# Gate projections: four of eight k pairs of the second column group in the 7-product form, and the pairs' weight sums ordered behind the sums read from PSUM

## The chip, the cores and the metric

The kernel runs on one core of one Trainium2 chip. The metric is the device time of one execution in microseconds (us). Engines are named as in the profile: PE is TensorE's matmul, PEld its weight load, DVE is VectorE, ACT is ScalarE, POOL is GpSimd and SP is SyncE. "L307" is line 307 of the kernel before.

## The reference

One residual block works on 256 rows of 2048 columns. What matters here is the combined input projection and its last 4096 columns, the two gates:

```python
h = rmsnorm(x, g_mix[i])
proj = h @ w_in[i]
q_sb, k_sb, v_sb, q_ca, k_ca, v_ca, gate_sb, gate_ca = jnp.split(proj, splits, axis=-1)
...
merged = (jax.nn.sigmoid(gate_sb) * (y_sb @ w_sb_out[i])
          + jax.nn.sigmoid(gate_ca) * (y_ca @ w_ca_out[i]))
x = x + merged @ w_mix_out[i]
```

Everything is float32. Attention, SwiGLU and a further projection follow and are not touched.

## The kernel before

**Products.** Each operand is split into a high part "hi" (a rounded copy) and a low part "lo" (what the rounding left). A product is three matmuls of 128x512 (hi by hi, hi by lo, lo by hi), all recorded at line 307 (`three`). ACT makes the high part with a cast (L277 for a single weight piece, L292 and L295 for the two pieces of a pair); DVE makes the low part with a subtraction. All of DVE's weight subtractions are recorded at L257 (`minus`).

**Units.** A unit is two column groups of 512 columns by 16 k tiles, that is 8 k pairs. Its order is a tuple of numbers. `i, i` means that k pair i is done as two single pieces (one for each column group, 12 matmuls each, 24 in all). `-i` means that k pair i is done for both column groups at once in the 7-product form (Strassen's and Winograd's way to multiply 2x2 blocks), which takes 21 matmuls. For that, `split_pair` makes weight sums: from two raw weight tiles DVE makes t3, the difference written back into raw, t2 and t4 (four subtractions of 128x512; t2, t3 and t4 lie in "xf"), then two low parts of 128x1024 and the low part of xf (128x1536, "T" or "room"); ACT makes two casts of 128x1024 and one of xf (128x1536, L298). Four of the seven products go to PSUM banks of their own ("su"). Behind the last pair `mid` reads them: a copy of one bank on ACT (L852) and four additions on DVE (L854). At the end of the unit `add_sums` adds the four "mm" banks (L858).

**The four units in a row.** `gate_unit` builds units that take no side tasks between their pieces. One stands alone, early (about 113 to 154 us of the trace). Four follow each other from about 252 to 423 us: A (two column groups of values, orders' entry 3), and B, C and D (the gates of column group c = 1, 2 and 3). B and C use entry 0, with pairs 2, 4 and 6 in the 7-product form; D uses entry 2, with four pairs. The early unit uses entry 1, with pairs 2, 4, 5 and 6:

```python
GATE_ORDERS = ((0, 0, 1, 1, -2, 3, 3, -4, 5, 5, -6, 7, 7), (0, 0, 1, -2, 1, -4, 3, -5, 3, -6, 7, 7),
               (0, 0, -2, 1, -4, 1, -5, 3, -6, 3, 7, 7),
               (0, 0, 1, 1, 2, 2, 3, 3, -4, 5, 5, -6, 7, 7))
```

**Buffers and order.** Raw weight tiles have five buffers and one more; SP loads them. The high and low parts have three rotating buffers each and a fourth ("hi_2459" and "lo_2460"). There is one xf. The units alternate between two sets of PSUM banks. `prefetch` splits pieces up to three ahead of the one being multiplied; `issue_after` adds an order between two instructions. A scheduler makes one fixed order for each engine from all this when the program is built, and each engine goes through its own list.

Of the kernel before, what the change touches and what calls it, by code (L numbers as in the profile page):

```python
# [12 lines left out]
ALU = mybir.AluOpType  # L13
# [6 lines left out]
D = 2048  # L20
KD = D // P
HEADS = 8
W = HEADS * P
# [8 lines left out]
NB = 512  # L32
# [20 lines left out]
def block_kernel(ctx: ExitStack, tc: tile.TileContext, x, p, w_in, w_sb_out, w_ca_out, w_mix_out,  # L53
# [18 lines left out]
    nc = tc.nc  # L72
# [101 lines left out]
    def unit(wsrc, n0s, kts, lhs, forms, ext, slots, mid, post, needs, row0=0, pairs=PAIRS, alone=None, after=None,  # L174
             order=None, seed=None):


        if alone is None:
            state["unit"] = state.get("unit", -1) + 1
        pool = state["unit"] % 2 if alone is None else alone  # L180
        g = dict(kind="unit", post=post, mid=mid, slots=slots, after=after, lhs=lhs, keep=None, forms=forms, ext=ext, pool=pool,
                 side=1 - pool, hold=alone is not None, seed=seed)
        kts = list(kts)
        if order is None:
            order = [j for i in range(len(kts) // 2) for j in ([-i] if i in pairs and i < len(kts) // 2 - 1 else [i, i])]
        taken = [-i for i in order if i < 0]
        begun = set()
        for i in order:
            own = i < 0
            i = abs(i)  # L190
            part = kts[2 * i : 2 * i + 2]
            r = (row0 + 2 * i) * P
            src = [wsrc[r : r + 2 * P, n0 : n0 + NB].rearrange("(k p) n -> p k n", p=P) for n0 in n0s]
            pc = dict(g=g, kts=part, ncol=NB, needs=[needs(kt) for kt in part])
            if own:
                pieces.append(dict(pc, src=src, pair=True, first=i == taken[0], last=i == taken[-1]))
            else:
                b = int(i in begun)
                begun.add(i)
                pieces.append(dict(pc, src=[src[b]], block=b, first=i == 0, last=2 * i + 2 == len(kts)))  # L200
# [26 lines left out]
    def load(pc):  # L227
        at = state["loaded"]
        pc["raw"] = []
        for src in pc["src"]:  # L230
            raw, dst = load_piece(src, pc["ncol"])
            pc["raw"].append(raw)
            state["raw"] += 1
            if at == 0:
                for k in range(2):
                    dma_w.dma_start(dst[:, k, :], src[:, k, :])
                continue
            if at in X_LOADS:
                with tc.issue_after(state["load"].ins):
                    load_x(X_LOADS.index(at))  # L240
            state["load"] = dma_w.dma_start(dst, src)
# [17 lines left out]
    def split(pc):  # L259
        for k in pc["needs"]:  # L260
            while k not in done:
                run_task()
        raws = pc.pop("raw")
        state["raw"] -= len(raws)
        for _ in raws:
            held.popleft()
        if pc["g"]["kind"] == "unit" and len(raws) == 2:
            return split_pair(pc, *raws)
        raw, = raws
        n = raw.shape[1]  # L270
        if pc["g"]["keep"] is None:
            hi, lo = buffers(n)
        else:
            hi, lo = (t[:, pc["kts"][0] * pc["ncol"] :][:, :n] for t in pc["g"]["keep"])
        m = n // 2 if pc is pieces[0] else n
        for c in range(0, n, m):
            state["cast"] = nc.scalar.copy(hi[:, c : c + m], raw[:, c : c + m])  # L277
            pc["split"] = minus(lo[:, c : c + m], raw[:, c : c + m], hi.bitcast(F32)[:, c : c + m])
        pc["hi"] = hi.rearrange("p (k n) -> p k n", n=pc["ncol"])
        pc["lo"] = lo.rearrange("p (k n) -> p k n", n=pc["ncol"])  # L280
# [120 lines left out]
    state = dict(loaded=0, split=0, at=0, raw=0, hl=0, ext=0, ps=ps_mm, fourth=None, ring=0, places=0, hold=False)  # L401
# [6 lines left out]
    def prefetch():  # L408
        while state["loaded"] < len(pieces) and state["raw"] + len(pieces[state["loaded"]]["src"]) <= RAW + state["places"]:
            load(pieces[state["loaded"]])  # L410
            state["loaded"] += 1
        room = 2 if state["at"] < 4 + KD // 2 else 4 if state["fourth"] is not None else 3
        while state["split"] < state["loaded"] and state["split"] <= state["at"] + 3:
            pc = pieces[state["split"]]
            if state["split"] > state["at"] and sum(map(size, pieces[state["at"] : state["split"] + 1])) > room:
                break
            behind = [started["p"]]
            if pc["g"] is pieces[4]["g"]:
                behind += started.get(pc["kts"][0] - 2, [])
            with ExitStack() as order:  # L420
                for i in behind:
                    order.enter_context(tc.issue_after(i.ins))
                split(pc)
            state["split"] += 1
# [11 lines left out]
    def flush(every=1, until=None, in_turn=False):  # L436

        n = 0
        while state["at"] < len(pieces) and (until is None or until not in done):
            pc = pieces[state["at"]]  # L440
            prefetch()
            products(pc)
            seed_next()
            state["at"] += 1
            n += 1
            if tasks and every and not state["hold"] and int(n / every) > int((n - 1) / every):
                if in_turn:
                    with tc.issue_after(state["mm"].ins):
                        run_task()
                else:  # L450
                    run_task()
# [393 lines left out]
    def gate_slots(c):  # L845
        return [gates[:, t, m, c * NB : (c + 1) * NB] for m in range(2) for t in range(NT)]

    def mid(g):

        q1, q5, q6, q7 = g["sums"]  # L850
        C = g["C"] = g["slots"]()
        nc.scalar.copy(C[0], q1)  # L852
        for i, q, j in ((2, q6, 0), (1, q7, 2), (3, q5, 1), (2, q5, 2)):
            nc.vector.tensor_tensor(C[i], q, C[j], ALU.add)  # L854

    def add_sums(g, b):
        for i in (2 * b, 2 * b + 1):
# [20 lines left out]
    def gate_unit(n0s, slots, post, order):  # L878
        pool = state["gate"] = 1 - state.get("gate", 0)
        unit(w2, n0s, range(KD), T1, lambda kt: F_gate[GATE_PAIRS.index(kt // 2)], [room[:, :3072], later_y[:, :3072]],  # L880
             slots, mid, post, hneed, alone=pool, order=GATE_ORDERS[order])
# [27 lines left out]
    gate_unit([columns(1, b) for b in range(2)], lambda: value_slots((1, 0)) + value_slots((1, 1)),  # L909
              add_values((1, 0), (1, 1)), 3)  # L910
    for c in range(1, 4):
        gate_unit([6 * W + m * D + c * NB for m in range(2)], lambda c=c: gate_slots(c), add_sums, 2 if c == 3 else 0)
    flush(None)
    state["fourth"] = None
    x_ = bp.tile([P, NT, D], F32, tag="x", name="x")
# [175 lines left out]
    for blk, nk in enumerate(FF_BLOCKS):  # L1091
        key = f"h{blk}"
        for c in range(nk // 4):
            j = k0 // 4 + c
# [127 lines left out]
```

## Time and profile before

| | |
|---|---|
| Time, median of 3 runs | 1456.28 us (1456.23 to 1456.53) |
| Profiled execution, its own time | 1455.66 us |
| Span of its trace | 1453.9 us (1.76 us lie outside the span) |
| PE busy / in the chain of work that ended last | 99% / 96% |
| DVE, PEld, ACT busy | 86%, 83%, 57% |
| Waits of PE on another engine in the whole trace | three, of 1.2, 0.4 and 0.3 us |

Matmuls are pipelined: one lasts 0.39 us in the records but the next starts 0.23 us later. DVE and ACT rows overlap in the same way by some hundredths of a microsecond, so distances here go from start to start.

### The profile page before, as it was taken

How to read it: one execution, taken by the hardware profiler on the slowest of the kernel's cores; microseconds unless marked ns; L12 is line 12 of the kernel's file. 1: busy time of each engine (PE TensorE's matmuls, PEld its weight loads, DVE VectorE, ACT ScalarE, POOL GpSimd, SP SyncE). 2: the span in 40 equal slices, each digit the busy share in tenths (PEclk: the TensorE clock that was granted, in tenths of full speed). 3: DMA queues.
4: the chain of work that ended last, by engine and by line, in shares of the span. 5: the costliest groups of instructions: out<-in, count | busy, mean ns of one | idle time of the engine just before them, and what ended most of it. 6: DMA issues, size and time to landing. Idle time of an engine off the chain costs nothing.

```text
span 1453.9 us, 18702 instructions
## 1 busy us (share of the span) xinstructions
PE 1443.5 (99%) x6837; PEld 1208.8 (83%) x6837; DVE 1249.7 (86%) x1587; ACT 829.6 (57%) x993; POOL 25.1 (2%) x44
## 2 busy tenths in 40 slices
PE   9999999999999999999999999999999999999997
PEld 7888888888888888888888888888888888888886
DVE  6979777898987767888999999999999989999785
ACT  6456555655545665555556655566655556666652
POOL 0200000000010000000000000000000000000100
PEclk9999999999999999999999999999999999999999
DMA  9866555666675655765666666666666666665871
GB/s 319 283 189 212 181 172 172 180 205 198 199 257 164 180 168 181 231 204 173 198 192 189 196 222 194 199 201 208 193 194 216 195 186 201 215 189 178 275 230 70
DMA packets 164731, 291.17 MB, mean 200 GB/s; under 512 B 9024, under 2 KB 42096, under 8 KB 164384
## 3 DMA queue, kind: packets, MB, share of 16 engines
q1 hardware_dynamic: 162528, 281.32, 62.0%
q0 software_dynamic: 2112, 8.68, 1.8%
q8 instruction: 53, 0.87, 0.2%
q14 instruction: 38, 0.31, 0.1%
HBM read 284.19 MB, written 5.77 MB: 199 GB/s over the span
## 4 chain that ended last, share of the span: by engine, by line
PE 96%; DVE 2%; DMA 1%; issue 1%; ACT 0%; DVEq 0%; SPq 0%; ACTq 0%
PE mm L307 67%; PE su L307 13%; PE mm L392 8%; PE mm L394 4%; PE tp L482 1%; DVE lo L257 1%; DMA raw<-in_w_in 1%; PE mml L307 0%; DMA raw<-in_w_ple_in 0%; PE mm L382 0%; PE xps L536 0%; DVE xf L257 0%; PE yp L709 0%; ACT hi L277 0%; PE wt L800 0%
## 5 line engine op out<-in xcount | busy, mean ns | idle before, releaser
L307 PE MATMUL mm<-hi,T 128*128 128x512 f32 x2650 | 854.6, 391 | 0.4 <-DVE v L854 0.4
L257 DVE TENSOR_TENSOR lo<-raw,hi 128x1024 fp32r<-128x1024 f32 (+1 forms) x517 | 625.1, 1221 | 121.9 <-ACT hi L277 113.0
L277 ACT CAST hi<-raw 128x1024 fp32r<-128x1024 f32 (+1 forms) x379 | 396.7, 1050 | 381.0 <-PE mm L307 257.8
L307 PEld LDWEIGHTS mm<-hi,T 128*128 128x128 f32 x2650 | 497.3, 188 | 103.0 <-issue 0.8
L307 PE MATMUL mm<-lo,T 128*128 128x512 f32 x1325 | 517.1, 391 | 0.0
L307 PEld LDWEIGHTS mm<-lo,T 128*128 128x128 f32 x1325 | 248.9, 188 | 50.7
L392 PE MATMUL mm<-T,hi 128*128 128x512 f32 x512 | 179.8, 398 | 0.0
L394 PE MATMUL mm<-T,lo 128*128 128x256 f32 x512 | 139.7, 280 | 0.0
L295 ACT CAST hi<-raw 128x1024 fp32r<-128x1024 f32 x69 | 72.7, 1053 | 76.2 <-DVE raw L257 29.5
L257 DVE TENSOR_TENSOR T<-xf,T 128x1536 fp32r<-128x1536 f32 x61 | 107.2, 1757 | 8.0 <-ACT T L298 7.2
L392 PEld LDWEIGHTS mm<-T,hi 128*128 128x128 f32 x512 | 94.6, 188 | 20.1
L257 DVE TENSOR_TENSOR xf<-raw 128x512 f32<-128x512 f32 x138 | 95.1, 689 | 13.2 <-DMA raw<-in_w_ffn_out 4.1
L394 PEld LDWEIGHTS mm<-T,lo 128*128 128x128 f32 x512 | 96.7, 189 | 2.3
L298 ACT CAST T<-xf 128x1536 fp32r<-128x1536 f32 x61 | 90.2, 1479 | 12.7 <-DVE xf L257 12.3
L292 ACT CAST hi<-raw 128x1024 fp32r<-128x1024 f32 x69 | 72.6, 1052 | 31.0 <-PE mm L307 20.5
L307 PE MATMUL mm<-T,T 128*128 128x512 f32 (+1 forms) x279 | 77.2, 371 | 0.0
L307 PE MATMUL su<-hi,T 128*128 128x512 f32 x170 | 66.1, 394 | 0.0
L307 PEld LDWEIGHTS mm<-T,T 128*128 128x128 f32 x279 | 49.3, 188 | 9.1
L854 DVE TENSOR_TENSOR C<-su,C 128x512 f32<-128x512 f32 x72 | 47.8, 686 | 0.4
L257 DVE TENSOR_TENSOR xf<-raw,xf 128x512 f32<-128x512 f32 x69 | 47.5, 689 | 0.5
L257 DVE TENSOR_TENSOR raw<-raw 128x512 f32<-128x512 f32 x69 | 47.5, 689 | 0.4
L307 PE MATMUL su<-T,FP 128*128 128x512 f32 x174 | 47.3, 389 | 0.0
(280 smaller groups left out, 1242.7 us busy)
## 6 DMA issues: line engine op xcount, KB each, us to landing
raw<-in_w_ffn_in SPq DMA_DIRECT2D x176, 512.0 KB, 4.1
raw<-in_w_in SPq DMA_DIRECT2D x160, 512.0 KB, 4.4
raw<-in_w_ffn_out SPq DMA_DIRECT2D x88, 512.0 KB, 4.4
raw<-in_w_mix_out SPq DMA_DIRECT2D x32, 512.0 KB, 4.6
raw<-in_w_ple_gate SPq DMA_DIRECT2D x32, 512.0 KB, 4.9
raw<-in_w_sb_out SPq DMA_DIRECT2D x16, 512.0 KB, 3.8
raw<-in_w_ca_out SPq DMA_DIRECT2D x16, 512.0 KB, 4.5
x<-in_x SPq DMA_DIRECT2D x4, 512.0 KB, 10.2
```

Of the source, the lines that this page charges most:

```text
L257: return nc.vector.tensor_tensor(out, a, b, ALU.subtract)
L277: state["cast"] = nc.scalar.copy(hi[:, c : c + m], raw[:, c : c + m])
L292: nc.scalar.copy(h1, raw1)
L295: nc.scalar.copy(h2, raw2)
L298: nc.scalar.copy(xh, xf)
L307: state["mm"] = nc.tensor.matmul(ps, u, v, start=first, stop=last, skip_group_check=True)
L392: nc.tensor.matmul(ps, hi[:, i, f], lhs[:, kt, :, :].rearrange("p c s -> p (c s)"), start=a, stop=False)
L394: nc.tensor.matmul(ps[:, :S], lo[:, i, f], lhs[:, kt, 0, :], start=False, stop=z)
L482: nc.tensor.transpose(ps[:, k, t * P : (t + 1) * P], src[:, t, (k0 + k) * P : (k0 + k + 1) * P], ident)
L854: nc.vector.tensor_tensor(C[i], q, C[j], ALU.add)
```

## The change

There are two edits. Line 912 gives unit B (c = 1) entry 1 of the orders in place of entry 0; C and D keep theirs. In `prefetch`, a pair of a `gate_unit` unit is issued behind `state["mid"]`, the last of `mid`'s additions that had been built by then. The order is between instructions of one engine, DVE.

```diff
@@ -417,6 +417,8 @@
             if pc["g"] is pieces[4]["g"]:
                 behind += started.get(pc["kts"][0] - 2, [])
+            if pc.get("pair") and pc["g"]["hold"] and "mid" in state:
+                behind.append(state["mid"])
             with ExitStack() as order:
@@ -851,7 +853,7 @@
         nc.scalar.copy(C[0], q1)
         for i, q, j in ((2, q6, 0), (1, q7, 2), (3, q5, 1), (2, q5, 2)):
-            nc.vector.tensor_tensor(C[i], q, C[j], ALU.add)
+            state["mid"] = nc.vector.tensor_tensor(C[i], q, C[j], ALU.add)
@@ -909,7 +911,7 @@
     for c in range(1, 4):
-        gate_unit([6 * W + m * D + c * NB for m in range(2)], lambda c=c: gate_slots(c), add_sums, 2 if c == 3 else 0)
+        gate_unit([6 * W + m * D + c * NB for m in range(2)], lambda c=c: gate_slots(c), add_sums, (0, 1, 0, 2)[c])
```

In the changed kernel L852, L854 and L858 are lines 854, 856 and 860. The lists of the engines differ from the end of A to the end of D and nowhere else. Three places follow; tile names carry buffer numbers that differ a little between the two programs.

**Place 1.** DVE at the end of unit A, before; "v" are the value tiles that A's sums go to, and the L257 rows on xf_2830, raw_2748 and raw_2746 are the weight sums of B's first pair.

```order
L257 TENSOR_TENSOR xf_2830<-raw_2748 128x512
L257 TENSOR_TENSOR lo_2779<-raw_2696,hi_2778 128x1024
L257 TENSOR_TENSOR raw_2748<-raw_2748,raw_2746 128x512
L854 TENSOR_TENSOR v_2740<-su_2645,v_2739 128x512
L257 TENSOR_TENSOR xf_2830<-raw_2748 128x512
L854 TENSOR_TENSOR v_2739<-su_2645,v_2740 128x512
L858 TENSOR_TENSOR v_2739<-mm0_2487,v_2739 128x512
L257 TENSOR_TENSOR xf_2830<-raw_2746,xf_2830 128x512
L854 TENSOR_TENSOR v_2740<-su_2644,v_2739 128x512
L854 TENSOR_TENSOR v_2740<-su_2644,v_2740 128x512
```

The same place of the changed kernel:

```order
L257 TENSOR_TENSOR lo_2779<-raw_2696,hi_2778 128x1024
L856 TENSOR_TENSOR v_2742<-su_2645,v_2741 128x512
L856 TENSOR_TENSOR v_2741<-su_2645,v_2742 128x512
L860 TENSOR_TENSOR v_2741<-mm0_2487,v_2741 128x512
L856 TENSOR_TENSOR v_2742<-su_2644,v_2741 128x512
L856 TENSOR_TENSOR v_2742<-su_2644,v_2742 128x512
L257 TENSOR_TENSOR xf_2813<-raw_2716 128x512
```

The four weight sums of B's first pair stood among the four additions and now begin behind the last of them.

**Place 2.** DVE in unit B of the changed kernel, at its second pair, k pair 4 (raw_2774, raw_2776, xf_2886); in the kernel before, unit B has its second pair later. The row lo_2944 belongs to the pair behind it, k pair 5.

```order
L257 TENSOR_TENSOR lo_2888<-raw_2774,hi_2887 128x1024
L257 TENSOR_TENSOR xf_2886<-raw_2776 128x512
L257 TENSOR_TENSOR lo_2900<-raw_2798,hi_2899 128x1024
L257 TENSOR_TENSOR raw_2776<-raw_2776,raw_2774 128x512
L257 TENSOR_TENSOR xf_2886<-raw_2776 128x512
L257 TENSOR_TENSOR lo_2944<-raw_2839,hi_2943 128x1024
L257 TENSOR_TENSOR xf_2886<-raw_2774,xf_2886 128x512
L257 TENSOR_TENSOR lo_2460<-raw_2776,hi_2459 128x1024
L257 TENSOR_TENSOR room_683<-xf_2886,room_683 128x1536
```

The low part lo_2944 of the next pair stands ahead of t4 (the last xf row) of this one.

**Place 3.** PE at the end of unit B of the changed kernel; mm_2800, mm_2826, su0_2861 and su1_2862 are B's banks and mm0_3111 is C's.

```order
L307 MATMUL su0_2861<-lo_3000,T1_71 128x512
L307 MATMUL su0_2861<-hi_2999,T1_71 128x512
L307 MATMUL mm_2800<-lo_3000,T1_71 128x512
L307 MATMUL mm_2800<-hi_2999,T1_71 128x512
L307 MATMUL mm_2826<-hi_3001,T2_72 128x512
L307 MATMUL su1_2862<-hi_3001,T2_72 128x512
L307 MATMUL mm0_3111<-hi_3065,T1_71 128x512
L307 MATMUL mm_2826<-lo_3002,T2_72 128x512
L307 MATMUL mm_2826<-hi_3001,T2_72 128x512
```

The matmul on mm0_3111, the first of unit C, stands ahead of 21 of B's; before, C's first matmul stood behind all of B's:

```order
L307 MATMUL mm_2817<-hi_2459,T1_71 128x512
L307 MATMUL mm0_3107<-hi_3061,T1_71 128x512
```

On ACT of the changed kernel, the cast that makes hi_3065 stands directly behind B's copy of su0_2861 (L854). In unit D, the four weight sums of the first pair stood among and ahead of C's additions and now begin behind the last of them; the other pairs of D follow them in the same sequence as before.

## Rows read from the trace of the kernel before

**Rows 1.** The page, parts 1 and 4: engines, and the last chain's shares.

```profile
PE 1443.5 (99%) x6837; PEld 1208.8 (83%) x6837; DVE 1249.7 (86%) x1587; ACT 829.6 (57%) x993; POOL 25.1 (2%) x44
PE 96%; DVE 2%; DMA 1%; issue 1%; ACT 0%; DVEq 0%; SPq 0%; ACTq 0%
```

**Rows 2.** The waits of PE, whole span: us, count, mean.

```profile
PE warm L580 <- POOL mhalf L108: 1.2, 1, 1.2
PE mm L307 <- DVE v L854: 0.4, 1, 0.4
PE mm L382 <- ACT hi L277: 0.3, 1, 0.3
```

**Rows 3.** Early unit, B, D: PE, PEld, DVE, ACT, POOL busy; clock, DMA share, GB/s.

```profile
108.00:153.00 45.00, 45.00 (x206) 37.41 (x205) 41.23 (x46) 23.09 (x23) 0.00 (x0) 1.00 0.71 222
298.60:340.20 41.60, 41.60 (x184) 34.45 (x185) 36.82 (x42) 23.24 (x24) 0.00 (x0) 1.00 0.64 196
381.70:422.50 40.80, 40.80 (x182) 33.79 (x181) 38.28 (x42) 21.18 (x20) 2.84 (x4) 1.00 0.67 208
```

**Rows 4.** The chain that ended last, one piece: start, length, count.

```profile
314.27 5.67 PE mm L307 x25
```

**Rows 5.** Timeline of PE, end of A and B's start: start, length, instruction.

```profile
297.79 0.39 PE L307 MATMUL mm<-hi,T 128*128 128x512 f32 x1
298.59 0.47 PE L307 MATMUL mm<-hi,T 128*128 128x512 f32 x1 [0.41 <-DVE v L854]
298.90 0.39 PE L307 MATMUL mm<-lo,T 128*128 128x512 f32 x1
...
306.63 0.62 PE L307 MATMUL mm<-hi,T 128*128 128x512 f32 x2
```

**Rows 6.** Timeline of DVE at the end of A.

```profile
294.22 0.69 DVE L257 TENSOR_TENSOR xf<-raw 128x512 f32<-128x512 f32 x1 [0.91 <-DMA raw<-in_w_in]
...
297.16 0.68 DVE L257 TENSOR_TENSOR xf<-raw 128x512 f32<-128x512 f32 x1
297.76 0.69 DVE L854 TENSOR_TENSOR v<-su,v 128x512 f32<-128x512 f32 x1
```

**Rows 7.** Timeline of ACT in B and D.

```profile
307.06 1.06 ACT L277 CAST hi<-raw 128x1024 fp32r<-128x1024 f32 x1 [1.55 <-PE mm L307]
...
322.97 1.48 ACT L298 CAST T<-xf 128x1536 fp32r<-128x1536 f32 x1 [0.57 <-DVE xf L257]
...
331.18 0.57 ACT L852 COPY gates<-su 128x512 f32<-128x512 f32 x1
331.65 1.05 ACT L277 CAST hi<-raw 128x1024 fp32r<-128x1024 f32 x1
...
392.33 1.05 ACT L277 CAST hi<-raw 128x1024 fp32r<-128x1024 f32 x1 [2.35 <-PE su L307]
393.28 1.48 ACT L298 CAST room<-xf 128x1536 fp32r<-128x1536 f32 x1
```

**Rows 8.** Timeline of DVE at the second pair of B.

```profile
321.11 1.23 DVE L257 TENSOR_TENSOR lo<-raw,hi 128x1024 fp32r<-128x1024 f32 x1 [0.16 <-ACT hi L277]
322.25 0.68 DVE L257 TENSOR_TENSOR xf<-raw,xf 128x512 f32<-128x512 f32 x1
...
324.48 1.76 DVE L257 TENSOR_TENSOR T<-xf,T 128x1536 fp32r<-128x1536 f32 x1 [0.41 <-ACT T L298]
326.16 1.22 DVE L257 TENSOR_TENSOR lo<-raw,hi 128x1024 fp32r<-128x1024 f32 x1
```

**Rows 9.** Timeline of DVE in D: first pair's first sum, C's last additions, second and fourth pair's last rows.

```profile
371.60 0.69 DVE L257 TENSOR_TENSOR xf<-raw 128x512 f32<-128x512 f32 x1 [0.31 <-DMA raw<-in_w_in]
...
381.02 1.28 DVE L854 TENSOR_TENSOR gates<-su,gates 128x512 f32<-128x512 f32 x2
...
394.79 1.76 DVE L257 TENSOR_TENSOR room<-xf,room 128x1536 fp32r<-128x1536 f32 x1 [0.15 <-ACT room L298]
...
410.64 1.75 DVE L257 TENSOR_TENSOR room<-xf,room 128x1536 fp32r<-128x1536 f32 x1
```

## Prediction

> **What bounds the kernel now.** I read the page first: PE is busy 99% of the span and holds 96% of the chain that ended last [rows 1]. The three waits of PE on another engine come to 1.9 us in all [rows 2]; so work taken from DVE or ACT gains nothing by itself, and what a change can gain is matmuls or one of these waits. One of the three lies at the edge of A and B: B's first matmul waited for an addition of A's sums [rows 2, 5]. The windows then show how thin the cover is: in B, DVE was busy 36.82 of 41.60 us, in D 38.28 of 40.80 us, and PE never waited [rows 3]. The granted clock is 1.00 throughout these windows [rows 3], the higher of its two levels, 2.4 GHz. A matmul takes 5.67 / 25 = 0.227 us from start to start [rows 4].
>
> So the question is whether the lists of DVE and ACT, in the changed order, still deliver each operand before PE comes to it. I answer it by walking the loops in the changed lists with distances from the rows.
>
> **The distances.** All are start to start or end to start.
> - From a matmul that reads a buffer last to the cast that reuses it: the third piece's last matmul began at 306.63, the cast at 307.06, so 0.43 us [rows 5, 7].
> - A cast of 128x1024 lasts 1.05 us and lets the next begin 0.95 us on (392.33 to 393.28); a copy of a bank lets the next cast begin 0.47 us on (331.18 to 331.65); the cast of xf lasts 1.48 us [rows 7].
> - On DVE a low part takes 1.14 us (321.11 to 322.25), a 128x512 row 0.60 us (297.16 to 297.76), and the low part of xf 1.68 us, with its end after 1.76 us [rows 6, 8].
> - t4's end (322.25 + 0.68 = 322.93) to xf's cast (322.97) is 0.04 us, and that cast's end (324.45) to DVE's row (324.48) is 0.03 us [rows 7, 8].
> - DVE's end to PE's start: the second addition ended at 297.76 + 0.69 = 298.45 and PE began at 298.59, so 0.14 us [rows 5, 6]. I use the same from ACT to PE, where no row stands alone.
> - A stop costs more than its length: the matmul behind the stop came 0.31 us after it (298.59 to 298.90), not 0.227, so 0.08 us on top [rows 5].
>
> **What goes away.** One more pair in the 7-product form takes 24 - 21 = 3 matmuls off, 0.68 us. The stop at the edge of A and B was 298.59 - 297.79 - 0.23 = 0.57 us, with the restart 0.65 us [rows 5]. In the changed list no weight sum stands between the first two additions any more, which brings the second one forward by at least 0.60 us (one 128x512 row), and the weight sum ahead of the first may go with it. Since 0.60 is over 0.57, I count the stop as gone: 0.68 + 0.65 = 1.33 us gained.
>
> **What DVE and ACT get.** DVE gets four rows of 128x512 and one of 128x1536, 4 x 0.60 + 1.68 = 4.08 us [rows 6, 8]; ACT gets one cast of xf, 1.48 us [rows 7]. Between nothing (hidden, as DVE was idle for 4.8 us of B's window [rows 3]) and 4.08 us, the loops decide where they show.
>
> **Four places where PE would wait.**
> 1. *B's second pair.* lo_2944 now stands ahead of t4 on DVE. Its cast needs the buffer that a single piece's last matmul frees, at T. Then cast begins at T + 0.43 and ends 1.05 later; lo 0.03 after it; t4 1.14 on, lasting 0.68; xf's cast 0.04 after, lasting 1.48; the low part of xf 0.03 after, lasting 1.76; PE 0.14 after. The sum is 6.78 us. PE has 25 matmuls queued behind T, 5.67 us. So it waits 1.11, with the restart 1.19 us.
> 2. *B's end.* C's first matmul stands ahead of 21 of B's. Its cast stands behind the copy of su0_2861, which needs the last matmul on that bank: 0.43 + 0.47 + 1.05 + 0.14 = 2.09 us. Five starts lie between, 1.13 us. The wait is 0.96, with the restart 1.04 us. Before, C's first matmul came behind all of B's, and 21 x 0.227 = 4.8 us covered the same chain.
> 3. *D's first pair.* Its first weight sum began at 371.60 and now stands behind C's last additions, which ended at about 382.2 [rows 9]: some 10 us of lead are gone. On ACT xf's cast stands behind a cast that waits for the first piece's buffer: 0.43 + 0.95 + 1.48 + 0.03 + 1.76 + 0.14 = 4.79 us against 19 matmuls, 4.31 us. The wait is 0.48, with the restart 0.56 us.
> 4. *D's third pair.* With no lead left, DVE's own work between two pairs decides: two pairs' sums (8 rows of 128x512), six low parts and two rows of 128x1536. From the second to the fourth pair of D, which is the same mix, it took 410.64 - 394.79 = 15.85 us [rows 9]; the changed list has one wait for xf's cast in it, and I take 16.0 us. PE needs 66 matmuls for this, 14.97 us. The wait is 1.03, with the restart 1.11 us.
>
> Together 1.19 + 1.04 + 0.56 + 1.11 = 3.90 us lost, 1.33 gained: 2.57 us slower. By the profiled execution that is a span of 1453.9 + 2.57 = 1456.5 us and a time of 1458.2 us; its 1455.66 lies 0.62 us under the median of the runs, and on the median it is 1456.28 + 2.57 = 1458.9 us. The bounds of this case: each loop's handovers could be off by some 0.1 to 0.2 us, which on four loops gives 1458.2 to 1460.0 us; the edge stop, if it stayed, would bring 0.65 us and lies inside.
>
> SP loads the same tiles in another order. The raw tiles of a pair are held longer when its sums begin later, so a load can come late: DVE waited 0.91 and 0.31 us for loads at B's and D's first pairs [rows 6, 9]. With those waits moved behind the additions, they should be gone; I cost them at nothing, and at most 0.91 us for a pair.
>
> The Trainium skill (Perfetto Trace Analysis, Identifying the Most-Contended Engine) says that occupancy is a fair measure for VectorE, that matmul busy time is none for TensorE, and that weight-load busy time should be taken there; by it DVE with 86% stands ahead of PEld with 83%, DVE is the engine to relieve, and the change loads it further. The trace agrees on the two shares, but not that DVE binds: PE waited for it once, 0.4 us [rows 1, 2].
>
> **The rivals.**
> - *No stop comes (the other side).* If buffers come free about 1.1 us earlier than in my loops, all four waits vanish, and 1.33 us are gained: 1455.0 us. For it: the early unit has the same order of pairs, and no wait of PE lies in it [rows 2, 3], with DVE 92% busy. Against it: there the row ahead of the second pair's t4 is a low part of that pair itself, whose cast comes earlier than the next pair's, and no such unit follows at its end. Past 0.96 us of error in loops 1 and 2, and 1.03 in 4, this decides; it also is what remains if the order edit is inert.
> - *Only B's two stops come*, since D keeps more lead than I give it: 1.19 + 1.04 - 1.33 = 0.90, 1457.2 us. For it: D's window has the highest DVE share, 94%, and PE still did not wait [rows 3].
> - *DVE binds through all of B to D*, so each microsecond that it gets shows: 4.08 - 0.68 = 3.4 us, 1459.7 us. Against it: DVE idled 4.8 us in B and 2.5 us in D [rows 3]. This is also what the skill's page cited above would lead to.
> - *Loads come late*, 0.91 us at three of the four changed pairs on top of my case [rows 6]: 1458.9 + 2.7 = 1461.6 us. Against it: DMA was busy 64 to 71% in these windows [rows 3].
>
> **How the numbers follow.** My case gets 0.60, no stop 0.18, B's stops only 0.12, DVE bound 0.07, late loads 0.03. The likeliest gives 1458.9 us, its own range 1458.2 to 1460.0. The range that takes in the other side goes from 1454.9 to 1460.2 us, since 0.18 lies at the low end and cannot be left out. A measurement of this kernel cannot tell less than about 0.2%, 2.9 us, from no change: from 1453.4 to 1459.2 us counts as the same. The most that can be gained is 1.33 us, 0.09%, so faster gets 0.01. Some 0.4 of my case lies above 1459.2 (0.24), nearly all of DVE bound (0.07) and late loads (0.03) too: slower 0.34, same 0.65.
>
> **What would show it.** In the changed trace: no wait of B's first matmul for A's additions; a wait of PE for the low part of xf (room) some 18 to 21 us into B; one for a cast on C's first matmul ahead of B's last 21; and two for room in D, 16 us apart. If DVE's t4 in B follows lo without PE waiting, loop 1 is wrong; if the first wait in D is missing, the 10 us of lead were not needed. The forecast fails if the buffers' reuse, which I read from the lists, does not bind as I walk it, or if new waits stand where I walked none.

## The result and the profile after

The changed kernel took 1458.58 us (median of 21 runs, 1457.82 to 1459.89) against 1456.18 us for the kernel before (21 runs, 1455.19 to 1457.59) on the same chip. The ratio is 1.0018, 95% interval 1.0012 to 1.0023: slower by 0.18%. The interval leaves out 1, so the change is slower, though by less than the bound of 0.2% that the prediction set for no change. Forecast were 1458.9 us, with 0.65 for the same and 0.34 for slower. The profiled execution took 1458.38 us, its span 1456.6 us.

The page of the changed kernel, parts 1 and 4; [rows 1] hold the same lines of before.

```profile
PE 1444.0 (99%) x6834; PEld 1207.6 (83%) x6834; DVE 1255.0 (86%) x1592; ACT 830.4 (57%) x994; POOL 24.8 (2%) x44
PE 97%; DVE 1%; ACT 1%; DMA 1%; issue 0%; SPq 0%; DVEq 0%; ACTq 0%
```

The waits of PE in the changed kernel, whole span; they answer to [rows 2].

```profile
PE su L307 <- DVE room L257: 1.4, 3, 0.8
PE warm L582 <- POOL mhalf L108: 1.2, 1, 1.2
PE mm L307 <- ACT hi L277: 0.7, 1, 0.7
PE mm L382 <- DVE pT L568: 0.4, 1, 0.4
PE mm L307 <- DVE lo L257: 0.3, 1, 0.3
```

The shares say little: none moved by more than a point. The waits say more. The one on A's additions is gone, and five new ones are there: three on "room" (the low part of xf), one on a cast and one on a low part. The waits at L580/L582 and L382 lie in the first ten microseconds and differ a little in every execution.

Busy times by stretch in the changed kernel, B, C and D, with the columns of [rows 3], which hold the windows of B and D before.

```profile
298.20:340.20 42.00, 40.70 (x177) 32.76 (x176) 39.17 (x43) 24.92 (x25) 0.00 (x0) 1.00 0.58 188
340.20:382.00 41.80, 41.80 (x186) 34.60 (x186) 38.40 (x44) 20.64 (x19) 0.00 (x0) 1.00 0.66 207
382.00:425.50 43.50, 42.37 (x186) 34.41 (x185) 41.82 (x46) 23.41 (x22) 2.85 (x4) 1.00 0.67 218
```

PE's busy time fell below the window's length in B and in D; DVE's rose from 36.82 of 41.60 to 39.17 of 42.00 us in B. The granted clock stayed at 1.00.

The timeline of PE in the changed kernel, the rows at its stops, with the row ahead of each where it stands alone; [rows 5] hold the stop of before.

```profile
316.08 0.39 PE L307 MATMUL su<-hi,T 128*128 128x512 f32 x1
316.75 0.50 PE L307 MATMUL mm<-lo,FP 128*128 128x512 f32 x1 [0.29 <-DVE lo L257]
317.09 0.39 PE L307 MATMUL mm<-hi,FP 128*128 128x512 f32 x1
...
318.25 0.39 PE L307 MATMUL mm<-room,T 128*128 128x512 f32 x1
318.93 0.96 PE L307 MATMUL su<-room,FP 128*128 128x512 f32 x3 [0.29 <-DVE room L257]
...
332.65 0.50 PE L307 MATMUL mm<-hi,T 128*128 128x512 f32 x1 [0.73 <-ACT hi L277]
332.98 0.40 PE L307 MATMUL mm<-lo,T 128*128 128x512 f32 x1
...
392.61 0.73 PE L307 MATMUL su<-room,FP 128*128 128x512 f32 x2 [0.28 <-DVE room L257]
...
408.75 0.73 PE L307 MATMUL su<-room 128*128 128x512 f32 x2 [0.85 <-DVE room L257]
```

Each stop is read as a distance from start to start, less the pace of 0.227 us. The first is 316.75 - 316.08 - 0.23 = 0.44 us, and the next matmul comes 0.34 us later, 0.11 over the pace: 0.56 us from unrounded starts. In the same way the five are 0.56, 0.56, 1.00, 0.55 and 1.12 us, together 3.79 us.

### The profile page after: what moved, and what is told of

Same layout as the page of the kernel before. It is cut to its first block, busy times and chain, and to the rows that moved or that the text cites. A ratio compares the mean times of both kernels' runs of the same rounds, so it can differ in the third digit from the quotient of the medians.

```text
span 1456.6 us, 18705 instructions
## 1 busy us (share of the span) xinstructions
PE 1444.0 (99%) x6834; PEld 1207.6 (83%) x6834; DVE 1255.0 (86%) x1592; ACT 830.4 (57%) x994; POOL 24.8 (2%) x44
## 4 chain that ended last, share of the span: by engine, by line
PE 97%; DVE 1%; ACT 1%; DMA 1%; issue 0%; SPq 0%; DVEq 0%; ACTq 0%
PE mm L307 69%; PE su L307 13%; PE mm L392 8%; PE mm L394 4%; PE tp L484 1%; DMA raw<-in_w_ple_in 1%; PE mml L307 0%; DVE room L257 0%; PE yp L711 0%; PE xps L538 0%; ACT hi L277 0%; PE wt L802 0%; DVE lo L257 0%; PE zp L701 0%; PE yp L701 0%; PE zp L699 0%
## 5 line engine op out<-in xcount | busy, mean ns | idle before, releaser
L257 DVE TENSOR_TENSOR lo<-raw,hi 128x1024 fp32r<-128x1024 f32 (+1 forms) x517 | 623.5, 1218 | 118.6 <-ACT hi L277 109.5
L257 DVE TENSOR_TENSOR T<-xf,T 128x1536 fp32r<-128x1536 f32 x62 | 108.7, 1753 | 9.4 <-ACT T L298 8.9
L257 DVE TENSOR_TENSOR xf<-raw 128x512 f32<-128x512 f32 x140 | 96.0, 686 | 12.2 <-DMA raw<-in_w_ffn_in 4.6
L257 DVE TENSOR_TENSOR xf<-raw,xf 128x512 f32<-128x512 f32 x70 | 47.9, 685 | 0.7
L257 DVE TENSOR_TENSOR raw<-raw 128x512 f32<-128x512 f32 x70 | 47.9, 684 | 0.4
```

What stands on the lines that cost most here:

```text
L257: return nc.vector.tensor_tensor(out, a, b, ALU.subtract)
```

## The experiments

All times stand beside runs of the kernel before on the same chip. Since the runs of one kernel spread over 1 to 2 us, the verdict on a place is read from PE's stops there, counted as above. The table lists them from the end of A to the end of D for every kernel but e8, e10 and e11. "By stops" is the sum of the stops, less 0.66 us of before, less 0.68 us where B has four pairs (three matmuls fewer).

| kernel | stops of PE, us | sum | by stops | measured against before |
|---|---|---|---|---|
| before | edge A-B 0.66 | 0.66 | | |
| changed | B's 2nd pair 1.12, C's first matmul 1.00, D's 1st pair 0.55, D's 3rd 1.12 | 3.79 | +2.45 | +2.40 |
| e1 order only | D's 1st 0.55, D's 3rd 1.12 | 1.67 | +1.01 | +1.42 |
| e2 sequence only | edge A-B 0.92, C's first 1.00 | 1.92 | +0.58 | +0.56 |
| e3 D free | B's 2nd 1.13, C's first 1.00, D's 3rd 1.30 | 3.43 | +2.09 | +2.07 |
| e4 low part behind t4 | B's 2nd 0.08, B's 3rd 0.54, C's first 1.00, D's 1st 0.55, D's 3rd 1.22 | 3.39 | +2.05 | +2.20 |
| e5 C behind B | B's 2nd 1.12, B's last 0.61, D's 1st 0.56, D's 3rd 1.13 | 3.42 | +2.08 | +2.05 |
| e7 three edits | B's 2nd 0.07, B's 3rd 0.56, B's last 0.73, D's 3rd 1.26 | 2.61 | +1.27 | +0.89 |
| e9 order for B alone, three pairs | none | 0.00 | -0.66 | -1.13 |
| e12 order for B alone, four pairs | B's 2nd 1.11, C's first 1.00, edge C-D 0.72, D's 3rd 0.79 | 3.61 | +2.27 | +1.08 |
| e13 e12 and two edits | B's 2nd 0.08, B's 3rd 0.52, B's last 0.73, D's 3rd 1.79 | 3.12 | +1.78 | +1.93 |

Two columns that were got in different ways agree within 0.5 us but for e12 (1.2 us off; its interval, 0.9996 to 1.0015, reaches to +2.2). The trace of e12 is that of its slowest execution, 1458.48 us against a median of 1457.23, and within this one execution the two agree: its span is 1456.5 us, 2.6 us over the 1453.9 of before, against 2.27 by stops. The other traces of the table agree with their own spans within 0.3 us, but for e5, whose trace was 1.1 us late already at A's first addition (297.20 us, 296.11 in the changed kernel). e10 and e11 fit as well: stops of 5.95 and 2.67 us, +4.61 and +1.33 by stops, +4.90 and +1.22 measured. So PE's stops in this stretch account for the change's effect.

**e1, the order edit alone.** Line 914 of the changed kernel (912 before) keeps `2 if c == 3 else 0` in effect; the diff shows the end of the line alone:

```diff
-... (0, 1, 0, 2)[c])
+... (0, 0, 0, 2)[c])
```

> The kernel before with the order edit alone: unit B keeps its three pairs. Walked loops: the wait at the edge of A and B (0.57 and 0.08 us) goes; D's two waits (0.55 and 1.12 us over the pace) come, since they hang on D's late start; B's waits at its second pair and at C's first matmul don't: 1456.2 - 0.65 + 1.67 = 1457.2 us. Backlog (DVE's whole list from B to D is what PE waits for, and a wait taken away comes back further on): DVE has 4.08 us less to do than in the changed kernel, so D's waits shrink or go: 1455.5 to 1456.5 us.

Measured: 1457.44 us against 1456.02, ratio 1.0009 (0.9999 to 1.0018). PE's timeline in e1 has two stops, both in D:

```profile
390.91 0.74 PE L307 MATMUL su<-T,FP 128*128 128x512 f32 x2 [0.27 <-DVE T L257]
...
407.08 0.74 PE L307 MATMUL su<-T,room 128*128 128x512 f32 x2 [0.84 <-DVE T L257]
```

They have the size of the changed kernel's (0.55 and 1.12 us), though DVE has 4.08 us less to do. So the order edit alone is enough for D's two waits; they need no backlog out of B.

**e2, the sequence alone.**

```diff
             if pc.get("pair") and pc["g"]["hold"] and "mid" in state:
-                behind.append(state["mid"])
+                pass
```

> The kernel before with four pairs in unit B and no added order. Walked loops: three matmuls fewer (0.68 us), the wait at the edge stays, D has its lead as before and does not wait; B's waits depend on the list that the scheduler makes, at most the 2.1 us of the changed kernel: 1455.5 to 1457.6 us. Backlog: the 4.08 us of work on DVE are there without the order edit too, so PE waits in B, and again at D's third pair by about 1 us, as it does in the changed kernel with D's pairs free: 1457.5 to 1458.6 us.

Measured: 1456.58 us against 1456.02, ratio 1.0003 (0.9994 to 1.0012): no change that can be told. The stop at the edge is there and longer than before (0.92 against 0.66 us), C's first matmul waits, and neither B's second pair nor D does. PE's timeline in e2, the two stops:

```profile
298.97 0.47 PE L307 MATMUL mm<-hi,T 128*128 128x512 f32 x1 [0.68 <-DVE v L856]
...
332.37 0.50 PE L307 MATMUL mm<-hi,T 128*128 128x512 f32 x1 [0.73 <-ACT hi L277]
```

So C's wait belongs to the sequence, and B's second pair waits only where both edits meet. The backlog's forecast, a wait of 1 us in D, failed.

**e4, the loop at B's second pair.** The next pair's first low part goes behind t4 of the pair ahead:

```diff
-        minus(t4, b[0][:, 1, :], t2)
+        last, state["t4"] = state.get("t4"), minus(t4, b[0][:, 1, :], t2)
         nc.scalar.copy(xh, xf)
-        minus(l1, raw1, h1.bitcast(F32))
+        with ExitStack() as order: last and pc["g"]["hold"] and order.enter_context(tc.issue_after(last.ins)); minus(l1, raw1, h1.bitcast(F32))
```

> The changed kernel, with the first low part of the next pair behind t4 of this pair on DVE (in unit B, and once in D). Walked loops: t4 no longer stands behind the cast that waits for PE's buffer; the path from T is then 0.43 + 1.05 + 0.03 + two low parts of 1.14 + 1.76 + 0.14 = 5.69 us against 25 matmuls, 5.67 us, so the two waits at B's second pair (0.56 us each over the pace in the changed kernel) shrink to under 0.15 us together, and the waits at C's first matmul (1.00) and in D (0.55 and 1.12) stay: about 1.0 us less, 1457.6 us. DVE bound: the same rows in another order, so no change, 1458.6 us. Late loads: no change either.

Measured: 1458.12 us against 1455.92, ratio 1.0014 (1.0005 to 1.0024). The stop at B's second pair fell from 1.12 to 0.08 us, as walked. But 0.54 us came back at B's third pair, where PE now waited for a low part (323.56, 0.27 us idle), and the sum of the stops fell by 0.40 us only. In the list the row that was moved was indeed the cause. What I missed shows in the timelines of DVE and of ACT in e4:

```profile
319.09 1.23 DVE L257 TENSOR_TENSOR lo<-raw,hi 128x1024 fp32r<-128x1024 f32 x1 [0.65 <-ACT hi L277]
...
322.29 1.22 DVE L257 TENSOR_TENSOR lo<-raw,hi 128x1024 fp32r<-128x1024 f32 x1
```

```profile
318.00 1.05 ACT L277 CAST hi<-raw 128x1024 fp32r<-128x1024 f32 x1 [2.08 <-PE su L307]
```

DVE was idle for 0.65 us until a cast had ended that itself waited for PE. From there five rows run close behind each other, and the last of them, at 322.29, is the low part that PE waited for. So what came up was the next loop from a buffer that PE frees, and not DVE's work alone.

**e8, the same loop made longer.** t4 of B's second pair is computed twice:

```diff
-        minus(t4, b[0][:, 1, :], t2)
+        for _ in range(1 + (pc["g"].get("c") == 1 and pc["kts"][0] == 8)): minus(t4, b[0][:, 1, :], t2)
```

> The changed kernel with t4 of B's second pair computed twice, the second time behind the pair's second low part. Walked loops: t4's chain from T grows by a low part and a row, 1.74 us, all of it in the loop, and the waits at B's second pair go from 1.12 to about 2.9 us; C's first matmul and D wait as before: 1460.3 us. DVE bound: one row more, 0.60 us: 1459.2 us.

Measured: one run, 1464.47 us. At B's second pair the stops came to 0.55 + 1.19 + 1.11 = 2.85 us, walked was 2.9; a single row on DVE, priced at 0.60 us, would not do that. The rest of the time is of another kind: the scheduler also made other lists for the end of B and for D. C's first matmul no longer waited, against the expectation, and PE stopped in D for 2.0 us (below, on the clock). The total of 1460.3 us was missed by 4 us for that.

**e5, the chain at C's first matmul.** PE's order alone is changed; the lists of DVE and ACT are untouched:

```diff
                 for t in range(2):
-                    row_products(...)
+                    order = tc.issue_after(state["mm"].ins) if g["hold"] and pc["first"] and pc["block"] + i + t == 0 else ExitStack()
+                    with order: row_products(...)
```

> The changed kernel, with C's first matmul ordered behind B's last on PE; DVE's and ACT's lists are the same row for row. Walked loops: 21 matmuls (4.8 us) cover the chain copy, cast, matmul of 2.09 us, so the wait of 1.00 us at C's first matmul goes and the four others stay: 1457.6 us. DVE bound: DVE's list is unchanged, so the wait comes back further on, in B's tail or in C: 1458.6 us. Late loads: unchanged, 1458.6 us.

Measured: 1457.97 us against 1455.92, ratio 1.0015 (1.0005 to 1.0024). C's first matmul no longer waits, but the next row does. PE's timeline in e5:

```profile
333.35 0.50 PE L307 MATMUL mm<-lo,T 128*128 128x512 f32 x1 [0.33 <-DVE lo L257]
333.68 0.40 PE L307 MATMUL mm<-hi,T 128*128 128x512 f32 x1
```

Of 1.00 us, 0.39 were won. The timeline of DVE in e5 shows why the rest was not: six rows close behind each other stand ahead of the low part that PE waited for, the first of the three at 332.07. The row of ACT makes the high part for the row of DVE at 330.33.

```profile
327.11 1.22 DVE L257 TENSOR_TENSOR lo<-raw,hi 128x1024 fp32r<-128x1024 f32 x1
328.25 0.69 DVE L257 TENSOR_TENSOR xf<-raw 128x512 f32<-128x512 f32 x1
...
330.33 1.23 DVE L257 TENSOR_TENSOR lo<-raw,hi 128x1024 fp32r<-128x1024 f32 x1
331.47 0.68 DVE L257 TENSOR_TENSOR xf<-raw,xf 128x512 f32<-128x512 f32 x1
332.07 3.49 DVE L257 TENSOR_TENSOR lo<-raw,hi 128x1024 fp32r<-128x1024 f32 x3
```

```profile
329.24 1.06 ACT L277 CAST hi<-raw 128x1024 fp32r<-128x1024 f32 x1 [2.89 <-PE mm L307]
```

So at the end of B C's cast was late by 1.0 us, and behind it a low part was late by 0.6 us. Two chains reach that low part at the same time. One is DVE's own rows, which leave no time to spare. The other is a loop of the kind walked above: the cast at 329.24 waited for PE to free its buffer and ended at 330.30, 0.03 us ahead of the row at 330.33. Which of the two binds was not separated, so the rival "DVE binds" may be true there in part, but it is not shown.

**e3, D's pairs free of the order edit.** `pieces[-1]["g"]["c"] = c` stands behind each `gate_unit` call, and

```diff
-            if pc.get("pair") and pc["g"]["hold"] and "mid" in state:
+            if pc.get("pair") and pc["g"]["hold"] and "mid" in state and pc["g"].get("c") != 3:
```

> The changed kernel, but D's pairs are not ordered behind C's additions. Walked loops: D has its lead of some 10 us back and both of its waits (0.55 and 1.12 us) go; B's and C's three stay: 1456.9 us. DVE bound: D's work on DVE is the same, so D's waits stay: 1458.6 us. Late loads: the first pair's sums wait for their load again on DVE (some 0.3 us, as before the change), hidden.

Measured: 1457.99 us against 1455.92, ratio 1.0012 (1.0003 to 1.0021). D's first stop went (0.55 us), the one at its third pair stayed (1.30 us). Half of the expectation failed: freeing D alone does not take the second wait away. The timeline of DVE in e3 has a wait for a load at D's first sum that in [rows 9] was 0.31 us:

```profile
373.80 0.69 DVE L257 TENSOR_TENSOR xf<-raw 128x512 f32<-128x512 f32 x1 [1.31 <-DMA raw<-in_w_in]
```

**e12, C's and D's pairs free.** The condition of e3 with `== 1` in place of `!= 3`.

> The changed kernel with the order edit for B's pairs alone; C's and D's are free. With D's pairs alone free its third pair still waited 1.19 us over the pace, and D's first sum waited 1.31 us for its load on DVE. If that came from C's ordered pairs, which hold their raw tiles longer, it goes here: the edge does not wait, B's three waits stay (2.12 us), D has none: 1458.6 - 1.67 = 1456.9 us. If it came from DVE's backlog out of B with four pairs, D's third pair still waits about 1.2 us: 1458.1 us.

Measured: 1457.23 us against 1456.15, ratio 1.0005 (0.9996 to 1.0015). D's third pair still waits, 0.79 us, and D's first matmul now waits for C's additions, 0.72 us: the stop of the edge A-B again, one unit edge further on. DVE's wait for the load at D's first sum is longer yet:

```profile
375.02 0.69 DVE L257 TENSOR_TENSOR xf<-raw 128x512 f32<-128x512 f32 x1 [3.01 <-DMA raw<-in_w_in]
```

So C's ordered pairs were not what made that load late, and my reading of e3 fell. Nor does it take four pairs in B: with three, e9 (below) has a wait of 1.24 us for the same load, and with four and no added order e2 has none. The load is late, by 1.2 to 3.0 us, in all five kernels in which B's pairs are ordered and D's are free (e3, e7, e9, e12, e13). In the traces SP issued it behind a row of DVE in unit C, at 366.83 us before, 369.13 in e3 and 368.73 in e12, and it landed 4.7, 4.6 and 6.2 us later. Why that row comes later, and why the load took longer in e12, was not separated. The late load alone does not make PE wait: e9 has it and no stop in D.

**e7 and e13, edits together.** e7 has the edits of e3, e4 and e5; e13 those of e12, e4 and e5.

> The three edits together: the next pair's first low part behind t4, C's first matmul behind B's last, D's pairs not ordered. The work on every engine is that of the changed kernel. Walked loops: all five waits (3.79 us over the pace) go but some 0.15 us, and what is left is the gain of the three matmuls and of the edge: 1456.2 - 1.3 + 0.15 = 1455.0 us, 0.1% under the kernel before. DVE bound: 1458.6 us, as the changed kernel.

> The order edit for B's pairs alone, with the next pair's first low part behind t4 and C's first matmul behind B's last. If C's ordered pairs were the cause of the waits in D: those (1.3 us with the three edits) go, B's two of 0.56 and 0.73 us at lines' low parts stay: 1456.1 - 1.33 + 1.3 = 1456.1 us, the time of the kernel before; the three matmuls are paid for by DVE's lateness at the end of B. If backlog out of B was the cause: 1457 us.

Measured: e7 1456.81 us against 1455.92, ratio 1.0006 (0.9997 to 1.0015); e13 1458.08 us against 1456.15, ratio 1.0009 (1.0001 to 1.0018). Both expectations failed: e7 kept 2.61 us of stops where 0.15 were expected, e13 3.12. In e13 PE waited at D's third pair for ACT's cast of xf (405.92, 1.13 us idle) and not for its low part. The walked loops price a list as it stands; they don't say what is left when the worst of them is taken away.

**e10 and e11, the first weight sum on POOL.** In B, C and D:

```diff
-        minus(t3, b[1][:, 1, :], b[1][:, 0, :])
+        (nc.gpsimd if pc["g"].get("c") else nc.vector).tensor_tensor(t3, b[1][:, 1, :], b[1][:, 0, :], ALU.subtract)
```

e10 is the changed kernel with this, e11 is e7 with this.

> The changed kernel with the first weight sum (t3, 128x512) of all eleven pairs of B, C and D on POOL, which is idle there: 11 x 0.60 = 6.6 us off DVE. No run shows what such a row takes on POOL. Walked loops: t3 is in none of the loops at B's second pair and C's first matmul, so their waits (2.1 us) stay; D's third pair gets 2 x 0.60 us back and no longer waits: 1457.5 us. Backlog: with 6.6 us off its list DVE is ahead everywhere, and most of the 3.79 us go: 1455 to 1456 us. Rows of DVE that become longer while POOL works would speak for a resource that the two share.

> The kernel with the three edits (median 1456.81 us, 2.61 us of waits left in this stretch) with t3 of B, C and D on POOL. Backlog: what waits are left there go: 1456.8 - 2.5 = 1454.3 to 1455 us, 0.1% under the kernel before. Walked loops: they forecast no such waits there in the first place; if the waits that are left come from ACT's casts or from loads and not from DVE's backlog, they stay: 1456.8 us.

Measured: e10 1460.92 us (four runs) against 1456.02, ratio 1.0035 (1.0021 to 1.0049), 2.5 us worse by the medians than the changed kernel against its own runs of before; e11 1457.24 us, ratio 1.0008 (0.9999 to 1.0017). Neither theory forecast e10. e11 lies near the 1456.8 us of the walked loops, but its stops do not: D's third wait is gone, and the one at B's last pair grew to 1.32 us (332.78). The test doesn't tell the two theories apart, since DVE was not relieved. Groups of e10, 290 to 425 us, with the low parts of the changed kernel as the last line, then the timeline of POOL at two places and that of DVE at the second:

```profile
L293 POOL TENSOR_TENSOR xf<-raw 128x512 f32<-128x512 f32 x11 | 21.2, 1931 | 325.8 <-DMA raw<-in_w_in 247.8 <-DVE T L257 39.2 <-DVE room L257 38.8
...
L257 DVE TENSOR_TENSOR lo<-raw,hi 128x1024 fp32r<-128x1024 f32 x51 | 66.8, 1331 | 6.2 <-ACT hi L277 5.8 <-ACT hi L292 0.3
...
L257 DVE TENSOR_TENSOR raw<-raw 128x512 f32<-128x512 f32 x11 | 7.5, 683 | 4.0 <-POOL xf L293 4.0
...
L257 DVE TENSOR_TENSOR lo<-raw,hi 128x1024 fp32r<-128x1024 f32 x52 | 62.4, 1220 | 5.6 <-ACT hi L277 4.4 <-ACT hi L292 1.1
```

```profile
308.56 2.21 POOL L293 TENSOR_TENSOR xf<-raw 128x512 f32<-128x512 f32 x1 [14.02 <-DVE T L257]
317.94 1.29 POOL L293 TENSOR_TENSOR xf<-raw 128x512 f32<-128x512 f32 x1 [7.16 <-DVE room L257]
```

```profile
317.98 2.32 DVE L257 TENSOR_TENSOR lo<-raw,hi 128x1024 fp32r<-128x1024 f32 x1
```

A row of 0.69 us on DVE takes 1.93 us on POOL on average: 1.29 us in three of the eleven, and 2.1 to 2.2 us in the eight that began while a low part ran on DVE. The low parts on DVE lasted 1331 ns on average against 1220 ns in the changed kernel, 51 x 0.11 = 5.7 us more, and DVE waited 4.0 us for POOL's sums: 9.7 us against the 6.6 taken off. The one at 317.98 lasted 2.32 us beside a POOL row of 1.29 us.

**e9, the order edit for B alone, with B's three pairs.** The edge without the rest:

```diff
-            if pc.get("pair") and pc["g"]["hold"] and "mid" in state:
+            if pc.get("pair") and pc["g"]["hold"] and "mid" in state and pc["g"].get("c") == 1:
...
-... (0, 1, 0, 2)[c])
+... (0, 0, 0, 2)[c]); pieces[-1]["g"]["c"] = c
```

> The kernel before (unit B with three pairs) with the order edit for B's pairs alone; C's and D's pairs are free. Walked loops: the wait at the edge goes (0.57 and 0.08 us), D keeps its lead and does not wait: 1456.1 - 0.65 = 1455.4 us, no wait of PE from A to D. Backlog: DVE's work is that of the kernel before, so the same.

Measured: 1455.02 us (1454.24 to 1455.36, 11 runs) against 1456.15, ratio 0.9989 (0.9980 to 0.9998). Busy times by stretch in e9, B and D:

```profile
298.60:340.20 41.60, 41.60 (x185) 34.48 (x184) 36.85 (x42) 23.65 (x24) 0.00 (x0) 1.00 0.60 190
381.70:422.50 40.80, 40.80 (x182) 33.84 (x181) 39.01 (x43) 20.52 (x20) 2.84 (x4) 1.00 0.66 213
```

PE has no gap in either, and none in between. By its stops it should gain 0.66 us; the 1.13 us measured hold that within the interval. It is the fastest of all kernels here: the useful part of the change is the order at one edge, A to B.

## Why the prediction was right

The time (1458.58 for 1458.9 us, 2.40 us slower for 2.57) and the mechanism held, step by step.

- **The stop at the edge goes, 0.65 us.** Right. DVE of the changed kernel, at the end of A; in [rows 6] the second addition began at 297.76:

```profile
296.11 1.42 DVE L856 TENSOR_TENSOR v<-su,v 128x512 f32<-128x512 f32 x2 [0.41 <-PE su L307]
```

  The second now ended at 296.11 + 1.42 = 297.53 us, 0.92 us sooner than 298.45, more than the 0.60 that I counted at least.
- **B's second pair, 1.19 us.** It measured 1.12, in two stops of 0.56. The loop ran as walked; here are its rows on ACT and then on DVE:

```profile
312.65 1.05 ACT L292 CAST hi<-raw 128x1024 fp32r<-128x1024 f32 x1 [2.34 <-PE mm L307]
...
315.60 1.48 ACT L298 CAST room<-xf 128x1536 fp32r<-128x1536 f32 x1 [0.94 <-DVE xf L257]
```

```profile
313.74 1.23 DVE L257 TENSOR_TENSOR lo<-raw,hi 128x1024 fp32r<-128x1024 f32 x1 [0.70 <-ACT hi L292]
314.88 0.68 DVE L257 TENSOR_TENSOR xf<-raw,xf 128x512 f32<-128x512 f32 x1
...
317.11 1.76 DVE L257 TENSOR_TENSOR room<-xf,room 128x1536 fp32r<-128x1536 f32 x1 [0.41 <-ACT room L298]
```

  With T = 312.65 - 0.43 = 312.22, PE's start at 318.93 is 6.71 us on; the walk said 6.78. The difference lies in the last distance: the low part of xf ended at 317.11 + 1.76 = 318.87 us and PE began 0.06 us later, where I had taken the 0.14 us of the edge. I had missed that PE waits first for the pair's second low part, which stands behind t4 too; it takes half of the same loss.
- **C's first matmul, 1.04 us:** 1.00. The rows of ACT are the copy and the cast of the walk; the cast ended at 332.60, and PE began at 332.65:

```profile
331.05 0.59 ACT L854 COPY gates<-su 128x512 f32<-128x512 f32 x1
331.55 1.05 ACT L277 CAST hi<-raw 128x1024 fp32r<-128x1024 f32 x1
```

- **D's first pair, 0.56:** 0.55. **D's third, 1.11:** 1.12. The rows are DVE's low parts of xf at the two places; they lie 16.15 us apart, where I had taken 16.0:

```profile
390.80 1.76 DVE L257 TENSOR_TENSOR room<-xf,room 128x1536 fp32r<-128x1536 f32 x1 [0.16 <-ACT room L298]
...
406.95 1.75 DVE L257 TENSOR_TENSOR room<-xf,room 128x1536 fp32r<-128x1536 f32 x1
```

  The sum of the four was 3.90, measured 3.79.
- **The restart** was taken at 0.08 us from the one stop of before; in the changed kernel it was 0.11 us (316.75 to 317.09 is 0.34).
- **Loads, at nothing.** Right for the changed kernel: the waits of 0.91 and 0.31 us for loads [rows 6, 9] are gone. Wrong as a rule: where B's pairs are ordered and D's are free, DVE waits 1.2 to 3.0 us for one load.
- **The rivals.** "No stop" and "B's stops only" fell with the five stops. "DVE binds" would have given 3.4 us for 2.4; e1 refutes it in D, where 4.08 us less work on DVE left both waits as they were. What came back in e4, e5 and e7 is not told apart there: in e4 and e5 a loop from a buffer that PE frees ends at the same row as DVE's own work. What does not hold up is something that the prediction assumes without saying it: that each loop stands alone. As a sum over the list as it was that did no harm; for every edit that takes one loop away it failed, by 0.6 us (e4, e5), 1.3 us (e3) and 2.5 us (e7) in the sum of the stops.

What stays open is why the load for D's first pair is late where B's pairs are ordered and D's are free, and what makes D's third pair wait in e3, e7, e12 and e13: e9, with three pairs in B, has the late load and no stop, and e2, with four and no order, has neither.

## What to carry to other kernels

In this kernel, with one engine busy 99% of the time, the engines' shares told nothing of the reordering. Walk each loop from the matmul that frees a buffer to the matmul that needs the result, and count the matmuls queued between. Here that priced a given list to a tenth of a microsecond for each stop, but not the list that a repair leads to: behind the worst chain stood the next, so test a repair by all the stops of the stretch and not by the one that it removes. An order that is wanted at one edge should be stated for that edge: here it took 0.66 us of stops away at one edge and brought 1.67 us of them in another unit.

## What the runs showed of the hardware

**POOL beside DVE.** In e10 a DVE subtraction with two inputs from memory lasted up to 2.32 in place of 1.22 us when a POOL subtraction ran beside it (rows above). The Trainium skill (SBUF — State Buffer, Who interferes with whom) says that a DVE instruction with two SBUF inputs contends with a GpSimd instruction that reads SBUF, and that the pair of ports that the two share is an exclusive lock. The rows agree, in either order: POOL began at 317.94 and lasted 1.29 us, and the DVE row that began 0.04 us behind it ended 1.10 us later than its usual length; the POOL row at 308.56 began 0.16 us behind a DVE row of 1.22 us (308.40) and lasted 2.21 in place of 1.29 us.

**The clock.** In e8 PE stopped in D for 395.88 - 393.64 - 0.23 = 2.0 us, and at the end of the stop the granted clock fell. PE's timeline in e8:

```profile
393.64 0.40 PE L307 MATMUL su<-hi,T 128*128 128x512 f32 x1
395.88 1.22 PE L307 MATMUL su<-room,FP 128*128 128x512 f32 x2 [1.84 <-ACT room L298]
```

Busy times by stretch in e8, after that stop and behind it:

```profile
396.60:402.80 6.20, 6.05 (x15) 4.24 (x14) 5.66 (x7) 2.52 (x2) 0.00 (x0) 0.51 0.56 176
403.30:406.00 2.70, 2.70 (x14) 2.23 (x13) 1.75 (x3) 1.05 (x1) 0.00 (x0) 1.00 0.63 214
```

The clock was at the lower of its two levels, 1.2 GHz, for some 6.8 us (0.50 from 395.80 to 402.60), and matmuls came 0.43 us apart; some 14 of them at 0.2 us more cost 2.8 us, more than the stop itself. None of the stops up to 1.3 us in the other kernels of the table was followed by this.
